# First stage of a hybrid block: weights in 256-column blocks, raw tiles in the input ring, state-space preparation moved forward

## The chip, the cores and the metric

The kernel runs on 1 core of one Trainium2 chip. The metric is the device time of one execution in microseconds; the median of the runs is compared. Engines are named as in the profile: PE (TensorE's matmuls), PEld (its weight loads), DVE (VectorE), ACT (ScalarE), POOL (GpSimd), SP (the engine that issues most DMAs; "SPq" is its queue).

## The reference

A decoder block on x (1024 tokens x 1024 channels) with 256 memory tokens. Cut to what matters here:

```python
u = rms_norm(h, norm_mix[l]);  proj = u @ w_in[l]
u_ssm, q, k, v, f_logit, gate_logits = jnp.split(proj, [...], axis=-1)   # u_ssm: 512 columns
y_ssm = gelu(s5_ssm(u_ssm, lam_re, lam_im, log_dt, b_re, b_im, c_re, c_im, d_skip))
# lam_bar = exp(lam * dt); b_bar = ((lam_bar - 1) / lam) * b; a scan over time; y = Re(C state) + D*u
...   # forgetting attention, gates, output projection
h = h + memory_cross_attention(rms_norm(h, norm_mem_q), rms_norm(mem, norm_mem_kv), w_mem_q, w_mem_kv, w_mem_o)
h = h + (silu(f_a) * f_b) @ w_ffn_out[l]
```

## The kernel before

All matmuls are done in three parts: each float32 operand is split into a rounded high part and the remainder (`split`, lines 177 to 179: a cast on ACT, then a subtraction on DVE, or on POOL where asked), and `mm3` (lines 166 to 170) adds high x high, high x low and low x high in PSUM.

The first stage, `stage_in`, does three things. It normalises two tiles of memory tokens ("m", "n") and eight tiles of x (128 tokens each), transposes them on PE (line 223) and splits the result into `mT` and `uT` (`turned`; its tiles are `mh`, `ml` and `uh`, `ul`). It multiplies the memory by `w_mem_kv`: keys transposed, one group of 128 columns at a time (K0 to K3), and values by two blocks of rows at a time (V0 to V3). And it multiplies x by the 512 state-space columns of `w_in`, transposed: four groups of 128 columns (q) by two halves of the tokens (h), the steps Uqh, each eight k-blocks of three matmuls. The results go to DRAM (`kv_d`, `u_d`).

Weights go through three steps. D*i* (`wget`) loads a tile of 128 x 1024 into one of two `raw` slots: for i = 0 to 3 all 1024 rows by 128 key columns, for 4 to 7 two row blocks by 512 value columns, for 8 to 11 (8, 9, a, b) all rows by 128 input columns. W*i* (`wsplit`) splits it into a pair `whi`, `wlo` (four slots of each; a "g" behind the step puts the subtraction on POOL). K, V or U reads it. The x tiles, memory tiles and gain rows share a ring of ten slots ("xt").

The state-space layer's preparation, class `S5`, is part of this stage. `load(0)` to `load(3)` are the steps L0 to L3: L0 loads lambda, the step sizes and the two C matrices, L1 loads the two B matrices and d_skip, L2 and L3 transpose lambda and C on PE. `prepare` is a generator whose parts are the steps P0 to P5: exponentials (P0), sine and cosine (P1), tables `la` and `ld` (P2), `bb` from B (P3), and `cb` and the d_skip product (P4). The scratch tiles of the sine, and `tb` of P3, share the two slots of the tag `craw` with the C matrices.

What sets the order: a list of steps, `ORDER_IN`, is written out by hand (F: fetch a tile, Q: sum of squares, R: root, S: scale, T: transpose half a tile, E: evacuate and split it, G: gain row, X: warm-up matmuls, u/k/v: outputs). It is the order of priority, not of execution. The framework's planner goes through the program with a time for each instruction of its own, and gives each engine and SP's queue a fixed order: of what is ready by its reckoning, what is listed first. Slots of a tag are waited for by semaphores. `B.behind(ins)` makes what is issued in its block, on the engine of `ins`, follow `ins` in that engine's order.

The second stage, `stage_ssm`, runs 32 gate columns of 24 matmuls on PE (`gate`, `gate_weights`, two blocks of weights for two column groups, loaded by `wblock`, line 153) and weaves the four quarters of the state-space layer between them: `turn_weights(q)` before column 4 + 7q (its transposes are line 1351), `states(q)` before 5 + 7q (line 1382, which reads `xg`, loaded at line 1375), `out(q)` before 9 + 7q. `weights(q)` makes `fre`, `fim` and `Gm` from `ld`, `la`, `bb` and `cT` on POOL and DVE (lines 1300 to 1319), and the doubling of `EC`, `ES` on POOL and, for the upper levels, DVE (lines 1332 to 1334).

Of the kernel before, what the change touches and what calls it, by code (L numbers as in the profile page):

```python
# [9 lines left out]
F32 = mybir.dt.float32  # L10
# [4 lines left out]
ALU = mybir.AluOpType  # L15
# [4 lines left out]
P = 128  # L20
D = 1024
L = 1024
NT = 8
GRP = 32
NH = 8
DH = 64
ML = 256
# [4 lines left out]
RAW = 1072  # L32
# [34 lines left out]
def f32(ap):  # L67
    return ap.bitcast(F32)
# [50 lines left out]
class Block:  # L119
# [55 lines left out]
            self.mm3(ps, wh[:, k0 + k, :], wl[:, k0 + k, :], rh, rl, k == 0, k == nk - 1)  # L175

    def split(self, hi, lo, src, pool_lo=False):
        self.A.copy(hi, src)  # L178
        (self.G if pool_lo else self.V).tensor_sub(lo, src, f32(hi))  # L179
# [46 lines left out]
    def turned(self, ps, b, act, t):  # L226
        for i in range(0, 4, act.kg):
            hi, lo = act.tok(4 * b + i, t, act.kg)
            self.split(hi, lo, ps[:, i * P:(i + act.kg) * P].rearrange("p (k c) -> p k c", k=act.kg))

    def norm_turn(self, xs, act, t):

# [101 lines left out]
def stage_in(B, xp, s5, x, mem, g_mix, g_kv, w_in, w_mem_kv, uT, u_d, kv_d):  # L334
# [14 lines left out]

    def fetch(t):  # L350
        tiles[t] = xtile()
        S.dma_start(tiles[t], mem[(t + 2) * P:(t + 3) * P, :] if t < 0 else x[t * P:(t + 1) * P, :])

    def gain_rows():

# [29 lines left out]
        ps[t, b] = B.turn(tiles[t], b, ("misc", "pv")[b])  # L385

    def evac(t, b):
        B.turned(ps.pop((t, b)), b, *((mT, t + 2) if t < 0 else (uT, t)))

    def wget(i):  # L390
        if i < 4:
            src = w_mem_kv[:, i * P:(i + 1) * P]
        elif i < 8:
            src = w_mem_kv[2 * (i - 4) * P:2 * (i - 3) * P, 512:1024]
        else:
            src = w_in[:, C_U + (i - 8) * P:C_U + (i - 7) * P]
        raw[i] = B.wpool.tile([P, RAW], F32, tag="raw", bufs=2, name="raw")[:, :D]
        raw["last"] = S.dma_start(raw[i].rearrange("p (k c) -> p k c", k=D // src.shape[-1]),
                                  src.rearrange("(k p) c -> p k c", p=P))

    def wsplit(i, pool):
        hl = [B.wpool.tile([P, WSLOT], F32R, tag=t_, name=t_)[:, :D] for t_ in ("whi", "wlo")]
        if i < 8:
            B.split(*hl, raw.pop(i), pool)
        else:

            B.split(*[t_.rearrange("p (k n g) -> p k n g", k=8, n=16) for t_ in hl],
                    raw.pop(i).rearrange("p (k g n) -> p k n g", k=8, g=8), pool)
        w[i] = [t_.rearrange("p (k c) -> p k c", k=2 if 4 <= i < 8 else 8) for t_ in hl]
# [719 lines left out]
class S5:  # L1129
# [9 lines left out]
    def load(self, part):  # L1139

        B, sp = self.B, self.sp
        lam_re, lam_im, log_dt, b_re, b_im, c_re, c_im, d_skip = self.raw
        V, T, S, ident = B.V, B.T, B.S, B.ident
# [4 lines left out]
        if part == 0:  # L1148
            self.rows = sp.tile([48, P], F32, name="prow")
            S.dma_start(self.rows[0:16, :], lam_re.rearrange("(j two) p -> j (two p)", two=2))  # L1150
            S.dma_start(self.rows[16:32, :], lam_im.rearrange("(j two) p -> j (two p)", two=2))
            self.ldr = sp.tile([48, 2], F32, name="ldr")
            S.dma_start(self.ldr[32:48, :], log_dt.rearrange("(j two) -> j two", two=2))
            self.craw = []
# [4 lines left out]
            return  # L1159
        if part == 1:  # L1160
# [15 lines left out]
        for t_, cr in zip(self.cT, self.craw):  # L1176
            ps = B.bank("misc")
# [4 lines left out]
                B.A.copy(t_[64 * two:64 * two + 64], pv[:, two])  # L1182

    def prepare(self):
        B, sp, bb, dbc, par = self.B, self.sp, self.braw, self.dbc, self.par
# [61 lines left out]
        V.tensor_mul(t1, xr, li)  # L1247
        V.tensor_sub(qi, qi, t1)
        V.tensor_mul(qi, qi, den)
        self.bb = [pt("bb_re", [16, 16]), pt("bb_im", [16, 16])]  # L1250
        tb = sp.tile([P, 256], F32, tag="craw", bufs=2, name="tb").rearrange("p (j n) -> p j n", j=16)
        bc = lambda q_: q_.unsqueeze(2).to_broadcast([P, 16, 16])
# [5 lines left out]
        V.tensor_add(self.bb[1], self.bb[1], tb)  # L1258
        yield

        self.cb = [pt("cb_re", [16, 2, 16]), pt("cb_im", [16, 2, 16])]
        for i in range(2):
            G.memset(self.cb[i], 0.0)
            for g in range(2):
                V.tensor_scalar(out=self.cb[i][64 * g:64 * g + 64, :, g, :], in0=self.cT[i][64 * g:64 * g + 64],
                                scalar1=1.0 if i == 0 else -1.0, scalar2=None, op0=ALU.mult)
# [5 lines left out]
        self.dm = dbc.rearrange("p (g m) -> p g m", g=GRP)  # L1272
        V.tensor_tensor(out=self.dm, in0=self.dm,
                        in1=msk.unsqueeze(1).to_broadcast([P, GRP, 16]), op=ALU.mult)

    def t2(self, name, bufs=1):
        return self.qp.tile([P, 512], F32, tag=f"q_{name}", bufs=bufs, name=name)
# [554 lines left out]
```

## Time and profile before

| | us |
|---|---|
| median of 3 runs (1605.04 to 1607.14) | 1605.51 |
| the profiled execution | 1608.0 |
| its span, first to last instruction | 1606.3 |
| PE busy in the span | 1549.5 |
| DVE, ACT, POOL busy | 1025.3, 657.7, 252.8 |
| mean granted clock of TensorE | 0.981 |

A row of a timeline has start, length, engine, line, operation, tiles out<-in, shapes and count; what stands in brackets is how long the engine stood idle before it and what ended that. A row of the waits has who waited, for whom, the total in us, how many times, and the longest. The chain of work is followed back from the last instruction of the stretch asked for; each piece has start, length and what it was.

### The profile page before, as it was taken

How to read it: one execution, taken by the hardware profiler on the slowest of the kernel's cores; microseconds unless marked ns; L12 is line 12 of the kernel's file. 1: busy time of each engine (PE TensorE's matmuls, PEld its weight loads, DVE VectorE, ACT ScalarE, POOL GpSimd, SP SyncE). 2: the span in 40 equal slices, each digit the busy share in tenths (PEclk: the TensorE clock that was granted, in tenths of full speed). 3: DMA queues.
4: the chain of work that ended last, by engine and by line, in shares of the span. 5: the costliest groups of instructions: out<-in, count | busy, mean ns of one | idle time of the engine just before them, and what ended most of it. 6: DMA issues, size and time to landing. Idle time of an engine off the chain costs nothing.

```text
span 1606.3 us, 20464 instructions
## 1 busy us (share of the span) xinstructions
PE 1549.5 (96%) x7323; PEld 1272.1 (79%) x7323; DVE 1025.3 (64%) x1850; ACT 657.7 (41%) x1179; POOL 252.8 (16%) x336
## 2 busy tenths in 40 slices
PE   8698989999999999999999999999999999999997
PEld 6587878898877668888888787888888888788886
DVE  7645563425678786767555687876776677565555
ACT  6432333332466564223335564333333333344342
POOL 2007545010121112320001210100100000000001
PEclk9898999999999999999999999999999999999999
DMA  7743344663022554538603168444455544796642
GB/s 241 139 104 65 80 132 107 134 169 64 2 49 53 125 139 140 182 116 271 229 1 106 53 221 297 151 151 157 157 165 162 164 151 147 271 391 226 196 157 105
DMA packets 197625, 239.82 MB, mean 149 GB/s; under 512 B 35386, under 2 KB 126426, under 8 KB 197012
## 3 DMA queue, kind: packets, MB, share of 16 engines
q1 hardware_dynamic: 190900, 222.80, 47.2%
q10 hardware_dynamic: 6624, 15.73, 2.5%
q8 instruction: 57, 0.93, 0.3%
q14 instruction: 44, 0.36, 0.1%
HBM read 164.56 MB, written 75.86 MB: 150 GB/s over the span
## 4 chain that ended last, share of the span: by engine, by line
PE 79%; DVE 6%; DMA 5%; issue 4%; POOL 3%; ACT 2%; SPq 1%; DVEq 0%; POOLq 0%; ACTq 0%
PE mm L886 15%; PE pv L886 7%; PE mm L168 7%; PE mm L170 7%; PE mm L169 7%; PE mm L1023 5%; PE sc L886 4%; PE sc L1023 4%; PE pv L1023 3%; PE sc L168 3%; PE sc L170 3%; PE sc L169 3%; PE misc L1023 2%; DMA raw<-in_w_in_dram 2%; PE pv L168 1%
## 5 line engine op out<-in xcount | busy, mean ns | idle before, releaser
L179 DVE TENSOR_TENSOR wlo<-raw,whi 128x1024 fp32r<-128x1024 f32 (+2 forms) x121 | 130.1, 1078 | 139.6 <-ACT whi L178 138.3
L178 ACT CAST whi<-raw 128x1024 fp32r<-128x1024 f32 (+2 forms) x124 | 116.4, 940 | 217.7 <-DMA raw<-in_w_ffn_in_dram 55.2
L168 PE MATMUL mm<-uh,whi 128*128 128x512 f32 x344 | 139.5, 405 | 2.9 <-ACT whi L178 2.8
L169 PE MATMUL mm<-ul,whi 128*128 128x512 f32 x344 | 137.5, 400 | 0.0
L170 PE MATMUL mm<-uh,wlo 128*128 128x512 f32 x344 | 136.9, 398 | 0.0
L179 DVE TENSOR_TENSOR ol<-or,oh 128x1024 fp32r<-128x1024 f32 x73 | 89.3, 1223 | 70.1 <-ACT oh L178 69.1
L178 ACT CAST oh<-or 128x1024 fp32r<-128x1024 f32 x73 | 76.8, 1053 | 102.6 <-PE pv L1023 33.7
L918 POOL TENSOR_TENSOR g<-a,c 128x512 f32<-128x512 f32 x22 | 35.5, 1613 | 392.1 <-ACT a L917 392.1
L168 PEld LDWEIGHTS mm<-uh,whi 128*128 128x128 f32 x344 | 66.6, 194 | 15.9 <-ACT whi L178 3.3
L170 PEld LDWEIGHTS mm<-uh,wlo 128*128 128x128 f32 x344 | 66.1, 192 | 14.9 <-DVE wlo L179 1.3
L1651 POOL TENSOR_TENSOR pl<-pf,ph 128x512 fp32r<-128x512 f32 (+1 forms) x32 | 37.8, 1181 | 245.9 <-DVE ph L1650 200.9
L169 PEld LDWEIGHTS mm<-ul,whi 128*128 128x128 f32 x344 | 66.4, 193 | 11.3
L197 POOL TENSOR_TENSOR r<-ms,mhalf 128x1 f32<-128x1 f32 x26 | 16.1, 621 | 353.2 <-DVE ms L193 344.0
L1648 ACT ACTIVATE pf<-sc 128x512 f32<-128x512 f32 (+1 forms) x96 | 46.5, 490 | 50.4 <-DVE sc L1644 30.5
L886 PE MATMUL pv<-S3h,we 128*128 128x512 f32 x176 | 58.1, 389 | 0.0
L168 PE MATMUL sc<-uh,whi 128*128 128x512 f32 x104 | 41.5, 399 | 0.0
L1023 PE MATMUL mm<-oh 128*128 128x512 f32 x106 | 41.2, 389 | 0.0
L1023 PE MATMUL mm<-ol,oh 128*128 128x512 f32 x106 | 41.2, 389 | 0.0
L1023 PE MATMUL mm<-oh,ol 128*128 128x512 f32 x106 | 41.2, 389 | 0.0
L170 PE MATMUL sc<-uh,wlo 128*128 128x512 f32 x104 | 41.0, 395 | 0.0
L169 PE MATMUL sc<-ul,whi 128*128 128x512 f32 x104 | 41.0, 394 | 0.0
L168 PE MATMUL mm<-yh,whi 128*128 128x512 f32 x104 | 40.8, 392 | 0.0
(585 smaller groups left out, 4561.6 us busy)
## 6 DMA issues: line engine op xcount, KB each, us to landing
or<-c_d SPq DMA_DIRECT2D x77, 256.0 KB
raw<-in_w_in_dram SPq DMA_DIRECT2D x22, 512.0 KB
wo<-in_w_ffn_out_dram SPq DMA_DIRECT2D x22, 512.0 KB
c_d<-g SPq DMA_DIRECT2D x44, 256.0 KB
t_d<-wo SPq DMA_DIRECT2D x44, 256.0 KB
or<-t_d SPq DMA_DIRECT2D x44, 256.0 KB
raw<-in_w_ffn_in_dram SPq DMA_DIRECT2D x20, 512.0 KB
rawb<-in_w_ffn_in_dram SPq DMA_DIRECT2D x20, 512.0 KB
```

The lines of the kernel that those rows point to most:

```text
L168: T.matmul(ps, lh, rh, start=first, stop=False)
L169: T.matmul(ps, lh, rl, start=False, stop=False)
L170: T.matmul(ps, ll, rh, start=False, stop=last)
L178: self.A.copy(hi, src)
L179: (self.G if pool_lo else self.V).tensor_sub(lo, src, f32(hi))
L197: self.G.tensor_tensor(out=r, in0=v, in1=self.mhalf[:, 0:n], op=ALU.pow)
L886: T.matmul(ps, l_[:, k, :], r_, start=first and k == 0 and i == 0, stop=k == 3 and i == 2, skip_group_check=True)
L918: G.tensor_mul(g[:, 512:], a1, c1)
L1023: T.matmul(ps, l_[:, gi], r_[:, 512:], start=n < 3 and p == 0 and k == 0 or n == 7 and p == 0 and k == 0, stop=p == NP - 1 and k == 2, ski ...
L1648: self.exp = A.activation(pf[:, off:], ps[:, off:], AF.Exp)
L1651: G.tensor_sub(pl[:, off:], pf[:, off:], f32(ph[:, off:]))
```

## The change

Four things are changed, all in the first stage.

- Key weights (D0 to D3) and input weights (D8 to Db) are loaded as blocks of 512 rows by 256 columns instead of 1024 rows by 128 columns. Two tiles together hold two groups of columns; `column` takes the k-block from the first or the second. Rows of a load are 1 KB instead of 512 bytes.
- The raw tiles of the input weights take slots of the x tiles' ring instead of the two raw slots.
- Each weight split carries an edge: its cast on ACT follows the cast of the evacuation listed last before it.
- L0 loads lambda and the step sizes alone, and follows the last x tile's load instead of a weight's; the C matrices move to L1. `cb` and the d_skip product follow the last operation of `bb` on DVE. `prepare` reads B later, so that it may be started before L1.

`ORDER_IN` is written anew:

```diff
-Fm g Fn X16 D0 G0 X6 Qm Qn Rm D1 Sm F1 Tm0 Rn Em0 Sn Tn0 F0 Tm1 W0 Q0 G1 Tn1 En0 F2 Q1 W1g En1 Em1 K0 D2 F3 K1 R0
-S0 T00 T01 k0 E00 Q2 W2g D3 E01 F4 F5 D4 S1 T10 Q3 W3 k1 D5 K3 K2 W4 E10 W5 F7 D6 R1 F6 k2 T11 k3 S2 Q4 V0 S3g T30
-E11 D7 Q5 T20 R2 T21 E21 E20 S4 E30 W6 W7 T40 V1 D8 D9 L0 S5 E40 W8 T31 V2 T41 E31 V3 Da T50 Q6 v T51 W9
-E51 U00 Q7 E41 R3 S6 u00 Db L1 T60 E50 S7 T61 T70 Wag E61 U10 L2 E60 P0 U20 u10 T71 E70 E71 u20 P1 U21 U11 Wb U30
-P2 u30 U31 u11 u31 U01 L3 u21 P3 P4 P5 u01
+Fm g Fn X16 D0 G0 X6 Qm Qn Rm D1 Sm F1 F0 Tm0 Rn Em0 Sn Tn0 F2 Tm1 W0 Q0 F3 G1 Tn1 En0 F4 Q1 W1g En1 Em1 K0 D2 F5 K1 R0
+S0 T00 T01 k0 E00 Q2 W2g D3 E01 F7 F6 L0 S1 T10 Q3 W3 k1 D4 K3 K2 D5 E10 W4 D8 D9 R1 k2 T11 k3 S2 Q4 W5 V0 Da S3g T30
+E11 D6 Q5 T20 R2 T21 E21 E20 S4 E30 D7 L2 T40 V1 S5 E40 W6 W7 T31 V2 Db L1 T41 E31 V3 W8 W9 T50 Q6 v U00 T51
+E51 Q7 E41 P0 R3 S6 u00 U10 T60 E50 S7 T61 u10 P1 T70 E61 Wa Wbg E60 T71 U20 E70 E71 u20 U21 P2 U11 L3 U30
+P3 u30 U31 u11 u31 U01 u21 P4 P5 u01
...
     def split(self, hi, lo, src, pool_lo=False):
-        self.A.copy(hi, src)
+        cast = self.A.copy(hi, src)
         (self.G if pool_lo else self.V).tensor_sub(lo, src, f32(hi))
+        return cast
...
     def evac(t, b):
-        B.turned(ps.pop((t, b)), b, *((mT, t + 2) if t < 0 else (uT, t)))
+        ps["turned"] = B.turned(ps.pop((t, b)), b, *((mT, t + 2) if t < 0 else (uT, t)))
...
         if i < 4:
-            src = w_mem_kv[:, i * P:(i + 1) * P]
+            src = w_mem_kv[512 * (i % 2):512 * (i % 2 + 1), 256 * (i // 2):256 * (i // 2 + 1)]
...
-            src = w_in[:, C_U + (i - 8) * P:C_U + (i - 7) * P]
-        raw[i] = B.wpool.tile([P, RAW], F32, tag="raw", bufs=2, name="raw")[:, :D]
+            src = w_in[512 * (i % 2):512 * (i % 2 + 1), C_U + 256 * (i // 2 - 4):C_U + 256 * (i // 2 - 3)]
+        raw[i] = xtile("raw") if i > 7 else B.wpool.tile([P, RAW], F32, tag="raw", bufs=2, name="raw")[:, :D]
...
     def wsplit(i, pool):
         hl = [B.wpool.tile([P, WSLOT], F32R, tag=t_, name=t_)[:, :D] for t_ in ("whi", "wlo")]
+        with B.behind(ps.get("turned")):
...
+    def column(i, o, act, h, out):
+        for k in range(8):
+            rh, rl = act.rhs(k, h)
+            wh, wl = [t_[:, k % 4, o * P:(o + 1) * P] for t_ in w[i + k // 4]]
+            B.mm3(out, wh, wl, rh, rl, k == 0, k == 7)
+
     def keys(h):
         ps["k", h] = B.bank("mm")
-        B.gemm_t(ps["k", h][:, :ML], *w[h], mT, 0, 8)
+        column(h // 2 * 2, h % 2, mT, 0, ps["k", h][:, :ML])
...
     def ssm_in(q, h):
         ps["u", q, h] = B.bank("mm")
-        B.gemm_t(ps["u", q, h], *w[8 + q], uT, h, 8)
+        column(8 + q // 2 * 2, q % 2, uT, h, ps["u", q, h])
...
     def params(i):
-        with B.behind(raw["last"] if i < 2 else None):
+        with B.behind(raw["last"] if i == 1 else tiles["last"] if i == 0 else None):
             s5.load(i)
```

More of the change, by code (lines that the diff above doesn't have):

```diff
@@ L228, in turned @@
             hi, lo = act.tok(4 * b + i, t, act.kg)
-            self.split(hi, lo, ps[:, i * P:(i + act.kg) * P].rearrange("p (k c) -> p k c", k=act.kg))
+            last = self.split(hi, lo, ps[:, i * P:(i + act.kg) * P].rearrange("p (k c) -> p k c", k=act.kg))
+        return last
     def norm_turn(self, xs, act, t):
@@ L351, in fetch @@
         tiles[t] = xtile()
-        S.dma_start(tiles[t], mem[(t + 2) * P:(t + 3) * P, :] if t < 0 else x[t * P:(t + 1) * P, :])
+        tiles["last"] = S.dma_start(tiles[t], mem[(t + 2) * P:(t + 3) * P, :] if t < 0 else x[t * P:(t + 1) * P, :])
     def gain_rows():
@@ L402, in wsplit @@
         hl = [B.wpool.tile([P, WSLOT], F32R, tag=t_, name=t_)[:, :D] for t_ in ("whi", "wlo")]
[L403 to L409, printed above, removed]
+        with B.behind(ps.get("turned")):
+            if i < 8:
+                B.split(*hl, raw.pop(i), pool)
+            else:
+                B.split(*[t_.rearrange("p (k n g) -> p k n g", k=8, n=16) for t_ in hl],
+                        raw.pop(i).rearrange("p (k g n) -> p k n g", k=8, g=8), pool)
+        w[i] = [t_.rearrange("p (k c) -> p k c", k=2 if 4 <= i < 8 else 4) for t_ in hl]
+    def column(i, o, act, h, out):
[3 more added lines that the diff above has]
+            B.mm3(out, wh, wl, rh, rl, k == 0, k == 7)
     def keys(h):
         ps["k", h] = B.bank("mm")
-        B.gemm_t(ps["k", h][:, :ML], *w[h], mT, 0, 8)
+        column(h // 2 * 2, h % 2, mT, 0, ps["k", h][:, :ML])
     def keys_out(h):
@@ L1153, in load @@
             S.dma_start(self.ldr[32:48, :], log_dt.rearrange("(j two) -> j two", two=2))
+            return
+        if part == 1:
             self.craw = []
@@ L1158, in load @@
                 self.craw.append(cr)
-            return
-        if part == 1:
             self.braw = [pt("b_re", [16, 16]), pt("b_im", [16, 16])]
@@ L1184, in prepare @@
     def prepare(self):
-        B, sp, bb, dbc, par = self.B, self.sp, self.braw, self.dbc, self.par
+        B, sp, par = self.B, self.sp, self.par
         V, A, G = B.V, B.A, B.G
@@ L1249, in prepare @@
         V.tensor_mul(qi, qi, den)
+        bb = self.braw
         self.bb = [pt("bb_re", [16, 16]), pt("bb_im", [16, 16])]
@@ L1257, in prepare @@
         V.tensor_tensor(out=tb, in0=bb[0], in1=bc(qi), op=ALU.mult)
-        V.tensor_add(self.bb[1], self.bb[1], tb)
+        last = V.tensor_add(self.bb[1], self.bb[1], tb)
         yield
@@ L1264, in prepare @@
             for g in range(2):
-                V.tensor_scalar(out=self.cb[i][64 * g:64 * g + 64, :, g, :], in0=self.cT[i][64 * g:64 * g + 64],
-                                scalar1=1.0 if i == 0 else -1.0, scalar2=None, op0=ALU.mult)
+                with B.behind(last):
+                    V.tensor_scalar(out=self.cb[i][64 * g:64 * g + 64, :, g, :], in0=self.cT[i][64 * g:64 * g + 64],
+                                    scalar1=1.0 if i == 0 else -1.0, scalar2=None, op0=ALU.mult)
         msk = pt("msk", [16])
@@ L1271, in prepare @@
                         channel_multiplier=1)
-        self.dm = dbc.rearrange("p (g m) -> p g m", g=GRP)
-        V.tensor_tensor(out=self.dm, in0=self.dm,
-                        in1=msk.unsqueeze(1).to_broadcast([P, GRP, 16]), op=ALU.mult)
+        self.dm = self.dbc.rearrange("p (g m) -> p g m", g=GRP)
+        with B.behind(last):
+            V.tensor_tensor(out=self.dm, in0=self.dm,
+                            in1=msk.unsqueeze(1).to_broadcast([P, GRP, 16]), op=ALU.mult)
     def t2(self, name, bufs=1):
```

## The prediction

> **What bounds the kernel now.** I read the page first, then the windows of busy time, then the waits of PE, and last the chain of work and the engines' timelines at each hole.
>
> ```profile
> span 1606.3 us, 20464 instructions
> ...
> PE 1549.5 (96%) x7323; PEld 1272.1 (79%) x7323; DVE 1025.3 (64%) x1850; ACT 657.7 (41%) x1179; POOL 252.8 (16%) x336
> ```
>
> PE is busy for 1549.5 of 1606.3 us, so an edit that leaves PE's work alone can win only PE's holes, and time in which PE runs below its clock. The windows below are cut at the holes of the first two stages; the columns are the stretch, its length, the busy time of each engine (with instructions), and then PE's granted clock, DMA share and GB/s.
>
> ```profile
> 19.70:51.00 31.30, 29.07 (x180) 25.50 (x180) 28.02 (x68) 20.36 (x40) 5.05 (x2) 0.95 0.65 177
> 51.00:59.17 8.17, 0.00 (x0) 0.03 (x1) 2.37 (x3) 4.31 (x5) 0.00 (x0) 0.71 0.38 88
> 59.17:64.71 5.54, 5.54 (x17) 4.71 (x18) 5.25 (x12) 2.25 (x6) 0.00 (x0) 0.50 0.81 189
> ...
> 69.66:72.36 2.70, 0.01 (x2) 0.04 (x1) 2.70 (x4) 0.86 (x2) 1.09 (x3) 1.00 0.92 110
> ...
> 77.55:79.48 1.93, 0.00 (x0) 0.03 (x1) 1.43 (x4) 0.37 (x1) 0.00 (x0) 1.00 0.92 223
> 79.48:114.10 34.62, 34.62 (x157) 28.41 (x158) 13.39 (x64) 7.84 (x14) 0.00 (x0) 1.00 0.42 96
> 114.10:136.94 22.84, 22.84 (x105) 18.40 (x102) 16.80 (x74) 7.74 (x13) 10.47 (x36) 1.00 0.45 116
> 136.94:139.75 2.81, 0.14 (x1) 0.14 (x2) 2.74 (x4) 1.35 (x2) 2.73 (x4) 1.00 0.00 0
> 139.75:143.13 3.38, 0.90 (x5) 0.50 (x4) 2.30 (x3) 0.58 (x1) 3.24 (x3) 0.50 0.20 78
> 143.13:150.00 6.87, 6.87 (x26) 6.30 (x27) 2.28 (x4) 0.58 (x1) 4.33 (x4) 0.50 0.00 0
> ...
> 201.17:205.32 4.15, 0.00 (x0) 0.03 (x1) 2.60 (x3) 1.39 (x3) 2.59 (x3) 0.91 0.96 363
> 205.32:211.50 6.18, 6.18 (x23) 5.60 (x24) 4.00 (x6) 3.12 (x9) 2.48 (x3) 0.51 0.33 122
> ```
>
> The first stage ends on PE at 114.10, where the last input column ends and the gates' matmuls begin. Inside it PE stands still for 8.17, 2.69 and 1.93 us. After the longest hole it runs 5.54 us at clock 0.50, so half of that, 2.77, is lost too. The second stage has two more places: 136.94 to 150.00 (idle 2.67 and 2.48; 0.90 and 6.87 us at half clock, lost 3.9), and 201.17 (4.15 idle, then 6.18 us at 0.51, lost 3.0). PE's waits name what ended each hole:
>
> ```profile
> PE misc L223 <- DVE ul L179: 10.1, 2, 8.2
> ...
> PE pv L1382 <- DMA xg<-u_d: 4.2, 1, 4.2
> PE pv L223 <- DVE xt L217: 2.7, 1, 2.7
> PE pv L1351 <- POOL fre L1302: 2.7, 1, 2.7
> ```
>
> The 8.2 is a transpose of an x tile that waits for VectorE to empty a bank. VectorE was not working then: the chain of work, and its own row, say what it stood behind.
>
> ```profile
> 44.26 10.57 DMA raw<-in_w_in_dram
> ...
> 54.86 1.91 ACT whi L178
> ...
> 72.19 6.10 DMA dbc<-in_d_skip_dram
> ...
> 78.31 0.69 DVE dbc L1273
> ```
>
> ```profile
> 56.80 1.89 DVE L179 TENSOR_TENSOR wlo<-raw,whi 128x1024 fp32r<-128x1024 f32 x1 [7.78 <-ACT whi L178]
> ```
>
> A raw slot came free at 44.26; only then could the input weight W8 be loaded, and it took 10.57 us. ACT's cast of it and VectorE's subtraction (7.78 idle) stood at the heads of their queues, with the x tiles' evacuations behind them. The 1.93 is the same with another load: VectorE's d_skip product waits for `dbc`, which landed at 78.29. So three of the holes are loads that came late, in front of work that was ready.
>
> **The loads move (stage 1).**
>
> ```profile
> 30.03 0.38 SPq L398 DMA_DIRECT2D raw<-in_w_mem_kv_dram  x1
> ```
>
> W8 to Wb get slots of the x tiles (the ring of ten, which serves them in turn as memory and x tiles are transposed) instead of the two raw slots; they no longer wait for W6 and W7. The order lists D8 and D9 just after D5, which SP could issue at 30.03, so they go out some 13 us earlier and the 10.57 lie beside the key and value matmuls. The evacuations are listed ahead, and every weight cast now carries an edge behind the last evacuation before it on ACT, so a late weight can't block an x tile again. The d_skip product goes behind the last `bb` operation. Removed: 8.17 + 2.77 + 2.69 + 1.93 = 15.6 us. The other 2.23 idle in 19.70:51.00 I leave. The eigenvalue loads pass D4 to D9 on SP. D4's raw slot is free only when POOL has split W2 (below: 23.22 + 2.39 us), so I put them at nothing; without that cover D4 would be late by the time that SP spends on them, a few us.
>
> What this gives back, each term with its ends:
>
> ```profile
> 9.69 1.04 ACT L178 CAST whi<-raw 128x1024 fp32r<-128x1024 f32 x1 [0.53 <-DMA raw<-in_w_mem_kv_dram]
> ...
> 16.71 0.58 ACT L178 CAST mh<-misc 128x512 fp32r<-128x512 f32 x1 [1.98 <-PE misc L223]
> 17.68 1.07 ACT L374 ACTIVATE junk<-xt 128x1024 bf16<-128x1024 f32 x1
> ...
> 20.42 0.58 PE L169 MATMUL mm<-ml,whi 128*128 128x256 f32 x1 [0.22 <-DVE ml L179]
> ...
> 23.22 2.39 POOL L179 TENSOR_TENSOR wlo<-raw,whi 128x1024 fp32r<-128x1024 f32 x1 [8.48 <-ACT whi L178]
> ...
> 44.29 0.71 PE L168 MATMUL sc<-whi,mh 128*128 128x512 f32 x2
> ...
> 46.40 0.37 ACT L178 CAST uh<-misc 128x256 fp32r<-128x256 f32 x1 [1.29 <-PE misc L223]
> ```
>
> 1. *Keys.* A key column now needs two tiles, W0 and W1, and their casts stand behind the first evacuations. W0 was cast at 9.69; from 16.71 ACT has to do two evacuations (0.58), two squares (1.07) and two casts (1.04), 5.4 us, and POOL's subtraction of W1 takes 2.39: W1 is ready at 24.5. The first half of K0 (12 matmuls, 20.42 to about 23) covers most of the wait. I take 1.5, between 0 and 4.1 (24.5 - 20.4).
> 2. *Values.* W6 and W7 now stand behind E40. V2 began at 44.29; if E40's cast stays at 46.40, W6 is ready 0.4 + 1.05 + 1.2 later, at about 49, which is 4.7 late; if the transpose comes as early as its scaled tile allows, nothing. I take 2.0.
> 3. *First input column.* U00 needs W8 and W9, a cast and a subtraction more (1.91 and 1.89 by the rows of W8). The second pair hides behind U00's first 12 matmuls. I take 1.0, between 0 and 3.8.
> 4. *Preparation beside the x tiles.* VectorE has spare time after 51 now, and less then. Its rows:
>
> ```profile
> 63.26 0.76 DVE L179 TENSOR_TENSOR ul<-pv,uh 128x256 fp32r<-128x256 f32 x2
> ...
> 70.94 1.27 DVE L217 SCALAR_TENSOR_TENSOR xt<-xt,r,gain 128x1024 f32<-128x1024 f32 x1
> ```
>
> ```profile
> 82.39:92.10 9.71, 9.71 (x45) 8.04 (x46) 8.86 (x59) 1.23 (x3) 0.00 (x0) 1.00 0.01 3
> 114.50:124.10 9.60, 9.60 (x46) 7.69 (x45) 9.29 (x31) 4.91 (x9) 1.24 (x4) 1.00 0.79 180
> ```
>
> Before U21 it must do two weight subtractions (3.8), seven evacuations (5.3), two scales (2.5) and about 2.2 of value evacuations and roots: 13.8. Step P0, which is the window 82.39:92.10 (two evacuations are in it, which I leave in), adds up to 8.86: 22.7 in all. The cover is U00, U10 and U20; four gate columns and little else fill 22.84, so a column is 5.5, three are 16.5, and with the transposes between them some 19. That is 3.7 over if all of P0 falls there, less if part of it fills VectorE's 3.3 us of idle time before 51 (28.02 busy of 31.30). I take 2.0, between 0 and 8.9.
>
> Stage 1 thus ends 15.6 - 6.5 = 9.1 us sooner, at about 105. PE's arithmetic is the same: the same eight columns of 24 matmuls.
>
> **The preparation moves (stage 2).**
>
> ```profile
> 114.58 0.28 DVE L270 TENSOR_SCALAR trg_k<-mt 128x224 f32<-128x224 f32 x1 [3.75 <-PE misc L1179]
> ...
> 132.24 0.29 DVE L1332 TENSOR_TENSOR d<-EC,trg_cs 128x128 f32<-128x128 f32 x1 [5.16 <-POOL ES L1334]
> ```
>
> ```profile
> 141.88 1.19 POOL L1302 TENSOR_TENSOR fim<-w,w 128x448 f32<-128x448 f32 x1
> ```
>
> The sine's first tile sits in a slot of `craw`, so it waits for the transposes of the C matrices (step L3), which stood at the very end of the stage. From 114.58 to 143.07 the chain to `fim` takes 28.5 us, and PE has gates for 22.84: hence the two holes. The new order puts L3 behind U11, three columns ahead of the end: 16.5 us. `fim` is then ready 12 us after the stage's end instead of 28.5, 10.8 before PE wants it. The C loads move behind Db on SP with those of B and d_skip, but Db itself, no longer waiting for W9's split, goes out earlier too. I take the whole 2.67 + 2.48 + 3.9 = 9.0; the ends are 0 (L3 planned where it was) and 9.0.
>
> The hole at 201 is a load as well:
>
> ```profile
> 193.04 1.51 SPq L153 DMA_DIRECT2D raw<-in_w_in_dram  x2
> 194.64 0.46 SPq L1375 DMA_DIRECT2D xg<-u_d  x1
> ```
>
> `xg` stood on SP behind two gate loads that waited for VectorE, which was late with the first quarter's states. Of 4.15 + 3.0 = 7.2 I take 2.9, since that lateness partly comes from the first hole; ends 0 and 7.2. Gate weights now get slots only when U31 and U01 are done: one column (5.5) hides a cast and two subtractions (3.4).
>
> **The sum.** 9.1 + 9.0 + 2.9 = 21.0. The profiled execution took 1608.0 us (span 1606.3 and 1.7 around it), so its like would take 1587.0. It lies 2.5 above the median of the runs, 1605.51, so I forecast 1584.5 for the median.
>
> A rule weighs on the give-backs. A hole of 2.67 us (from 136.94) was enough here: from 139.75 on the clock is 0.50 for 10.25 us. The leftovers of 1 to 2 us I count without it. The Trainium skill (TensorE: Matmul & The Clock Gate, Part 1) gives half rate only after an idle window of about 3.4 us, and by it none of these leftovers could cost more than itself. By the trace one of them might, for up to 5.1; that end goes into the range.
>
> **Rivals.** *VectorE becomes the bound* (0.22). The loads are early, but P0 to P2 all stand ahead of the last evacuations: 8.9 + about 10 (the second window, its weight subtraction out, and the tables) against the 5.6 that the cover leaves. U21 waits 13 us, stage 1 wins nothing or loses 2, and the gain is stage 2's: 1605.5 - 9 = 1596. For it: 28.02 of 31.30 busy before 51. Against: P1 waits for L3, listed behind U11.
>
> *Slower* (0.16): the same place, with the doubling. If the planner also puts the first quarter's doubling ahead of the last evacuations, VectorE stands in order for POOL's part (5.16 in the row at 132.24), and runs the upper levels itself until about 142, 9.9 more. With P0, P1, P2 and `bb` (8.9, 10 and 3) that is 37 us ahead of U21; 31 of it PE waits, and 5 more are lost at half clock. Stage 1 then loses 25 and stage 2 wins 12: 1605.5 + 13 = 1618.5. It turns to a loss from about 24 us of preparation in front.
>
> *Nothing in sum* (0.05): the casts' edges bring back the stall in stage 1 and the S5 chain shifts with the stage: 1605.
>
> **How the numbers follow.** The forecast has 0.57. All bounds at their best give 15.6 + 2.2 + 9.0 + 7.2 = 34, that is 1571. Upward the range takes in the second case and a half clock on top of it, 1601. Slower and nothing, together 0.21, are left out. A difference under 0.2%, 3.2 us, can't be told from none. Faster 0.79, within 0.2% 0.05, slower 0.16.
>
> **What would show it.** Right: no wait of ACT for `raw<-in_w_in` in stage 1, no hole over 3 us between 20 and 105, the first `sc` gate matmul at about 105, L1351 without a wait, `xg` issued closer behind the first quarter's output. Wrong: PE L223 waiting for VectorE at 70 to 80 (rival one), or VectorE's L1332 ahead of the last `ul` (rival two), or the sine (L270) still at the stage's end.

## The result: 7 us faster, a third of what was forecast

| | us |
|---|---|
| before, median of 5 runs (1605.04 to 1607.14) | 1605.51 |
| after, median of 5 runs (1597.25 to 1600.66) | 1598.55 |
| ratio after/before, 95% interval | 0.9957 [0.9942, 0.9971] |
| forecast (range) | 1584.5 (1571 to 1601) |
| profiled execution, before and after | 1608.0 and 1598.55 |

The direction was right and the time lies in the range, but the size was not: 7.0 us came where 21 were expected. The page of the kernel after:

```profile
span 1596.8 us, 20467 instructions
...
PE 1542.6 (97%) x7323; PEld 1265.9 (79%) x7323; DVE 1026.5 (64%) x1850; ACT 657.1 (41%) x1179; POOL 254.3 (16%) x336
```

To see where the time went, both traces are cut at the same three marks of the program: the last input column's end, the first quarter's and the third quarter's `xg` matmuls. The first stage is cut besides at 19, 48 and 66 us of each trace. Windows of busy time, before:

```profile
19.00:48.00 29.00, 26.32 (x172) 23.41 (x170) 27.14 (x64) 21.00 (x41) 5.05 (x2) 0.94 0.61 187
48.00:66.00 18.00, 9.82 (x39) 7.96 (x38) 9.03 (x23) 6.83 (x11) 0.00 (x0) 0.72 0.68 143
66.00:114.29 48.29, 43.67 (x202) 35.42 (x201) 23.10 (x77) 14.62 (x25) 3.81 (x4) 1.00 0.55 107
...
114.10:154.10 40.00, 34.84 (x154) 28.73 (x152) 27.96 (x85) 10.26 (x16) 24.27 (x47) 0.87 0.30 76
154.10:254.46 100.36, 95.87 (x481) 81.50 (x480) 49.51 (x72) 34.53 (x56) 54.15 (x106) 0.97 0.50 117
```

And after, the same columns:

```profile
19.00:48.00 29.00, 21.88 (x136) 19.96 (x135) 26.41 (x59) 20.51 (x42) 8.17 (x3) 0.82 0.65 203
48.00:66.00 18.00, 15.51 (x69) 12.16 (x69) 16.81 (x39) 10.68 (x18) 0.00 (x0) 0.91 0.89 208
66.00:116.63 50.63, 47.00 (x210) 38.02 (x209) 28.93 (x128) 13.73 (x24) 4.64 (x3) 0.97 0.21 63
...
116.63:146.58 29.95, 29.95 (x146) 25.16 (x145) 12.18 (x15) 9.64 (x13) 23.85 (x53) 1.00 0.46 128
146.58:245.56 98.98, 94.52 (x482) 80.49 (x481) 56.85 (x83) 34.65 (x56) 52.92 (x102) 0.98 0.51 117
```

The second stage gave what was forecast: from its first gate to the third quarter it took 40.00 + 100.36 = 140.4 us before and 29.95 + 98.98 = 128.9 after, 11.4 less (forecast 11.9). The first stage gave nothing: the first gate comes at 116.6 instead of 114.3, where about 105 was forecast. (The profiled executions lie 9.5 apart, the medians 7.0.)

For the first stage I count what PE loses after 19 us in each part: its idle time (length less busy time), and half of its busy time inside the stretches at clock 0.50. The PEclk column is a mean that takes in idle time, so it falls lower than this second number alone would make it.

| lost, idle + half clock (us) | 19 to 48 | 48 to 66 | 66 to the end | sum |
|---|---|---|---|---|
| before | 2.7 + 1.6 | 8.2 + 2.7 | 4.6 + 0 | 19.8 |
| forecast for after | 5.8 | 3.0 | 2.0 | 10.8 |
| after | 7.1 + 4.2 | 2.5 + 1.7 | 3.6 + 1.7 | 20.8 |

The forecast's line is the line of before, less the 15.6 that go, plus the 6.5 of the give-backs, each in its part. The old stall at 48 to 66 did go. The new losses stand in front of it and behind it. Who was waited for, by PE's waits after (19 to 230 us):

```profile
PE pv L1439 <- ACT Tt L1383: 2.8, 1, 2.8
PE mm L170 <- POOL wlo L179: 2.8, 1, 2.8
PE sc L168 <- ACT whi L178: 2.3, 1, 2.3
PE pv L1396 <- DMA xg<-u_d: 1.6, 1, 1.6
PE mm L168 <- ACT uh L178: 1.4, 1, 1.4
PE misc L224 <- DVE rt L203: 1.4, 1, 1.4
PE mm L168 <- ACT whi L178: 1.2, 1, 1.2
```

No load stands here but `xg`. `Tt` and `xg` belong to the second stage; of the first stage's five rows three are weights being split (`wlo`, `whi`), 6.3 us of 9.1. Behind them, from the timelines of ACT, POOL and SP:

```profile
31.28 1.05 ACT L178 CAST whi<-raw 128x1024 fp32r<-128x1024 f32 x1
...
54.99 5.80 ACT L178 CAST whi<-raw 128x1024 fp32r<-128x1024 f32 x4
...
77.51 3.79 ACT L178 CAST whi<-raw 128x1024 fp32r<-128x1024 f32 x2
81.18 0.40 ACT L178 CAST uh<-misc 128x256 fp32r<-128x256 f32 x1
```

```profile
32.41 3.42 POOL L179 TENSOR_TENSOR wlo<-raw,whi 128x1024 fp32r<-128x1024 f32 x1 [7.80 <-DMA raw<-in_w_in_dram]
```

```profile
35.86 0.39 SPq L401 DMA_DIRECT2D raw<-in_w_mem_kv_dram  x1
```

The cast at 31.28 is W2, held by its edge until E00 is done. Its low part ends at 35.8, only then is its raw slot free, and D4 goes out at 35.86; before, W2's subtraction ended at 25.6 (the row at 23.22 in the prediction) and D4 followed it. W6 to W9 come as four casts in one piece at 54.99, behind E40. At 77.51 two casts with their edge satisfied stand in front of an evacuation (81.18): the block that the edges were to prevent, the other way round.

### The profile page after: what moved, and what is told of

Same layout as the page of the kernel before. It is cut to its first block, busy times and chain, and to the rows that moved or that the text cites. A ratio compares the mean times of both kernels' runs of the same rounds, so it can differ in the third digit from the quotient of the medians.

```text
span 1596.8 us, 20467 instructions
## 1 busy us (share of the span) xinstructions
PE 1542.6 (97%) x7323; PEld 1265.9 (79%) x7323; DVE 1026.5 (64%) x1850; ACT 657.1 (41%) x1179; POOL 254.3 (16%) x336
## 4 chain that ended last, share of the span: by engine, by line
PE 80%; DVE 7%; issue 4%; DMA 3%; POOL 3%; ACT 2%; SPq 1%; DVEq 0%; POOLq 0%; ACTq 0%
PE mm L897 15%; PE pv L897 7%; PE mm L168 7%; PE mm L170 7%; PE mm L169 7%; PE mm L1034 5%; PE sc L897 4%; PE sc L1034 4%; PE sc L169 3%; PE sc L170 3%; PE sc L168 3%; PE pv L1034 3%; PE misc L1034 2%; PE pv L168 1%; PE pv L170 1%
## 5 line engine op out<-in xcount | busy, mean ns | idle before, releaser
L169 PEld LDWEIGHTS mm<-ul,whi 128*128 128x128 f32 x344 | 65.6, 191 | 11.3
L1668 DVE TENSOR_TENSOR pl<-pf,ph 128x512 fp32r<-128x512 f32 (+2 forms) x64 | 35.1, 550 | 10.2 <-ACT ph L1667 9.4
L1129 POOL TENSOR_TENSOR sg<-sg,ga 128x512 f32<-128x512 f32 x16 | 29.4, 1858 | 73.4 <-DVE sg L1122 73.4
```

The source lines that it names most:

```text
L169: T.matmul(ps, lh, rl, start=False, stop=False)
L1129: self.B.G.tensor_mul(self.out[j][:, cs], self.out[j][:, cs], ga)
L1668: V.tensor_sub(pl[:, off:], pf[:, off:], f32(ph[:, off:]))
```

## The experiments

Theory A was that the edges cost what the loads gave; rival B the 256-column blocks (two tiles for each key column); rival C the preparation on VectorE, ahead of the last x tiles. Ratios are to the kernel before in the same runs.

**1. The edges off**, in the kernel after:

```diff
-        with B.behind(ps.get("turned")):
+        with B.behind(None):
```

> The changed kernel without the edge that puts a weight's cast behind the last evacuation (no weight has it). Theory A (the edges ate the gain of stage 1): W0 is cast near 10 us again and W2 near 23 instead of 31.28, D4 is issued near 26 instead of 35.86, the holes at 33.12 (2.8) and 53.83 (2.3) and the half clocks after them go, stage 1 ends near 108 instead of 116.8: about 1590 us. Theory B (the 256-column blocks cost it, because a key column now needs two tiles): the hole at 33 stays whatever the order on ACT is, 1597 to 1599. Theory C (VectorE is the bound of stage 1): the holes move but their sum stays, 1596 to 1600.

Measured: 1594.97, ratio 0.9935 [0.9921, 0.9948]; the interval overlaps that of after. First gate at 110.75, parts 4.4 + 4.1, 2.9 + 1.7, 3.0 + 0, sum 16.0 against 20.8. So the edges cost about 4.8 us in the profile and 3.6 in the median, less than half of the 8.5 that theory A gave. A wait of 3.0 for VectorE stays at 74.5, in the last part:

```profile
66.00:110.75 44.75, 41.79 (x196) 34.30 (x195) 28.98 (x117) 10.37 (x22) 3.69 (x3) 1.00 0.18 48
```

**2. L3 alone**, in the kernel before (the token L3 behind U11):

```diff
-... P1 U21 U11 Wb U30 P2 u30 U31 u11 u31 U01 L3 u21 P3 P4 P5 u01
+... P1 U21 U11 L3 Wb U30 P2 u30 U31 u11 u31 U01 u21 P3 P4 P5 u01
```

> The kernel before with one token of the order moved: step L3 (the transposes of the C matrices) directly behind U11 instead of behind U01. Theory (the whole gain of the change is the earlier sine): stage 1 ends at 114 to 115 as before, the two waits of PE for fre and fim go, and the time is about 1596, 9 to 10 less than the kernel before. Rival (the C loads, B loads or the edges behind bb are needed for it as well): a wait for fim of over 2 us stays and less than 4 us are won, over 1601.

Measured: 1591.58, ratio 0.9912 [0.9898, 0.9925]. One moved token gives twice what the whole change gives, and 4 us more than was expected of it. The windows: no wait from the stage's end to the first quarter, and 126.7 us to the third quarter's `xg`, against 140.4 before.

```profile
112.78:142.70 29.92, 29.92 (x145) 25.16 (x145) 11.76 (x15) 8.70 (x12) 27.69 (x56) 1.00 0.38 104
142.70:239.46 96.76, 93.97 (x481) 80.36 (x481) 54.01 (x79) 34.75 (x56) 50.24 (x100) 0.98 0.53 121
```

**3. The ring's slots alone**, in the kernel before:

```diff
-        raw[i] = B.wpool.tile([P, RAW], F32, tag="raw", bufs=2, name="raw")[:, :D]
+        raw[i] = xtile("raw") if i > 7 else B.wpool.tile([P, RAW], F32, tag="raw", bufs=2, name="raw")[:, :D]
```

> The kernel before with one line changed: the raw tiles of the input weights in the x tiles' ring, blocks, order and edges as before. Theory (the load of W8 was the long hole): it is issued near 36 instead of 44.26, ACT does not wait for it, the hole of 8.17 us and the half clock after it go, stage 1 ends near 104; the sine moves with the stage's end, so the waits for fre and fim stay: about 1595. Rival (VectorE is the bound of stage 1): other holes take its place, stage 1 ends at 110 or later, over 1601.

Measured: 1602.93, ratio 0.9984 [0.9975, 0.9993], over 1601, as the rival had it. But the stage ends at 108.75, between the theory's 104 and the rival's 110 and 5.5 sooner than before. The sine still sits at its end, so the second stage's waits move along with it and stay. The third quarter's mark comes 5.8 sooner and the profiled execution is 7.1 shorter, but the median only 2.6: one profile against another is no better than that.

**4. Edges on the input weights only**, in the kernel after:

```diff
-        with B.behind(ps.get("turned")):
+        with B.behind(ps.get("turned") if i > 7 else None):
```

> The changed kernel with the edge on the input weights alone (W8 to Wb); key and value weights are free. Theory A (the edges on key and value weights ate the gain): as without any edge, about 1590; if the edge on the input weights does its work, not slower than without it. Theory B (256-column key blocks) and theory C (VectorE): 1596 to 1600.

Measured: 1600.06, ratio 0.9969 [0.9955, 0.9983]; parts 4.4 + 4.3, 2.9 + 1.7, 3.6 + 1.7, sum 18.6. In the first two parts it is the run without edges, in the last it is the kernel after: so with the edges on W8 to Wb 5.3 are lost behind 66 instead of 3.0, and those on W0 to W7 make about 2.2 ahead of it. Theory A had 1590 here and fails: the time is clear of run 1's and not below that of after, so by the times the edges on the input weights cost all that edges cost, and those on W0 to W7 nothing that shows.

**5. L3 and the slots together**: the edits of runs 2 and 3, in the kernel before.

> The kernel before with two parts of the change and no other: step L3 directly behind U11, and the raw tiles of the input weights in slots of the x tiles' ring. Alone, L3's place took 13.9 us off the time, and the slots took 5.4 us off the first stage and 2.6 off the whole. Theory A (the gains are these two, and what eats them are the edges and the order around them): the gains add, since with L3 early the second stage starts without a wait wherever the first stage ends; first gate matmul near 109, time 1591.6 - 4 = 1587.5, within 1586 to 1590. Rival (the slots' gain is taken back behind the first stage whatever the sine does): 1591, as with L3 alone.

Measured: 1590.88, ratio 0.9911 [0.9895, 0.9927]: as with L3 alone. The gains did not add in the median, though the first gate comes at 110.4 in the profile, against 113.3 in run 2; the clock in that profile is looked at in the last section.

**6. 128-column blocks again**, without the edges:

```diff
-            src = w_mem_kv[512 * (i % 2):512 * (i % 2 + 1), 256 * (i // 2):256 * (i // 2 + 1)]
+            src = w_mem_kv[:, i * P:(i + 1) * P]
...
-            src = w_in[512 * (i % 2):512 * (i % 2 + 1), C_U + 256 * (i // 2 - 4):C_U + 256 * (i // 2 - 3)]
+            src = w_in[:, C_U + (i - 8) * P:C_U + (i - 7) * P]
...
-        column(h // 2 * 2, h % 2, mT, 0, ps["k", h][:, :ML])
+        B.gemm_t(ps["k", h][:, :ML], *w[h], mT, 0, 8)
...
-        column(8 + q // 2 * 2, q % 2, uT, h, ps["u", q, h])
+        B.gemm_t(ps["u", q, h], *w[8 + q], uT, h, 8)
```

> The kernel after without the edges, and with the key and input weights in 128-column blocks again. Against the kernel after without the edges alone (1594.97, first gate matmul at 110.6, keys' end at 33.8). Theory A (the blocks cost little: a key column waits for two tiles once): keys end about 1.5 earlier, time within 1592 to 1596. Theory B (the 256-column blocks are what the change pays, since each column needs two casts and two subtractions): stage 1 ends at 106 to 107, time 1590 to 1591.

Measured: 1594.95, ratio 0.9938 [0.9922, 0.9955], the same as run 1. Rival B falls by the time: the part 19 to 48 loses 6.6 instead of 8.5, but 48 to 66 loses 8.3 instead of 4.6, and the first gate comes at 113.9, 3.2 later than in run 1.

**7. The edges alone**, in the kernel before:

```diff
+        with B.behind(ps.get("turned")):     # around both branches of the split
             if i < 8:
                 B.split(*hl, raw.pop(i), pool)
```

> The kernel before with the edges alone: each weight's cast follows the cast of the evacuation listed last before it. Theory A (the edges hold back casts of weights that have landed, and through the two raw slots the loads behind them): keys and values end later than before (35.5 and 51.0), by 3 to 10 us, the input weights load later, and the time is 1608 to 1615. Rival (an edge costs only where the order of the list puts it late, as with W2 in the new list): in the old list W2 also stands behind E00, but W4 to W9 behind E10 to E41; no measurable difference, 1604 to 1607.

Measured: 1613.03, ratio 1.0044 [1.0028, 1.0059]: 7 us slower by the ratio, as theory A said. The first gate comes at 123.7. D4 goes out at 37.8 instead of 25.6, and all loads behind it with it; ACT then waits 6.0 us for D8. PE's waits:

```profile
PE pv L224 <- DVE rt L202: 5.6, 1, 5.6
PE mm L168 <- ACT whi L178: 4.0, 1, 4.0
PE mm L169 <- DVE ul L179: 3.1, 1, 3.1
```

**8. P0 and P1 listed behind E71**, without the edges:

```diff
-E51 Q7 E41 P0 R3 S6 u00 U10 T60 E50 S7 T61 u10 P1 T70 E61 Wa Wbg E60 T71 U20 E70 E71 u20 U21 P2 U11 L3 U30
+E51 Q7 E41 R3 S6 u00 U10 T60 E50 S7 T61 u10 T70 E61 Wa Wbg E60 T71 U20 E70 E71 u20 P0 P1 U21 P2 U11 L3 U30
```

> The kernel after without the edges, and with the steps P0 and P1 (exponentials, sine and cosine) listed behind the last x tile's evacuation instead of ahead of the scales of tiles 6 and 7. Against the kernel after without the edges alone (1594.97; PE waits 3.0 us for VectorE's ul at 74.5). Theory C (VectorE is the bound there: P0 stands in front of the x tiles): the wait at 74.5 goes, stage 1 ends at 107 to 108, time 1591 to 1592. Theory A (the wait is the weight subtractions of W8 to Wb, not P0): the wait stays between 2 and 3.5, time 1594 to 1596, or later if the sine is then late for the second stage.

Measured: 1596.25, ratio 0.9944 [0.9929, 0.9959]. By its times this looks like theory A, but the edit had not done what it says: the timeline of VectorE has P0's last operation still in front of the subtraction that PE waits for.

```profile
75.45 0.17 DVE L1226 TENSOR_TENSOR em<-em,e 128x16 f32<-128x16 f32 x1
75.54 0.42 DVE L179 TENSOR_TENSOR ul<-misc,uh 128x256 fp32r<-128x256 f32 x1
```

A list of priorities moves nothing that is ready by the planner's reckoning while what should pass it is not. So run 8 says nothing on theory C, and it was made again with an edge. The new list did shift losses all the same: 48 to 66 loses 2.2 instead of run 1's 4.6, and behind 66 it is 7.6 instead of 3.0.

**9. The preparation held behind E71 on VectorE**, with run 8's list and without the weights' edges:

```diff
+        ps["low"] = B.low        # the evacuation's subtraction on VectorE
...
+    def prepare():
+        with B.behind(ps.get("low")):
+            next(prep, None)
```

> The kernel after without the edges on the weights, P0 and P1 listed behind the last x tile's evacuation, and the preparation's operations on VectorE held behind that evacuation's subtraction by an edge of their own: the list alone (the run before of this kind) had left them ahead of it, from 69.7 to 76.0. Theory C (P0 on VectorE is what PE waits for): the hole of 3.0 to 4.7 us at 72 to 77 goes or falls under 1, the first gate matmul comes at 107 to 108 instead of 110.6, and since VectorE then stood idle for 14 us before the sine, nothing is late behind it: 1591 to 1592.5. Theory A (the wait is the weight subtractions of Wa and Wb): a hole over 2 stays, 1594 to 1596.

Measured: 1587.39, ratio 0.9887 [0.9871, 0.9903], clear of run 1's interval, and faster than both kernels. Windows:

```profile
19.00:48.00 29.00, 24.64 (x146) 21.82 (x147) 24.71 (x62) 17.36 (x37) 5.24 (x2) 0.83 0.73 193
48.00:66.00 18.00, 15.84 (x76) 12.23 (x75) 17.71 (x32) 14.53 (x20) 2.74 (x1) 1.00 0.92 220
66.00:106.06 40.06, 39.92 (x188) 32.75 (x187) 29.32 (x130) 9.82 (x21) 2.05 (x3) 1.00 0.19 50
```

Behind 66 PE stands for 0.14 us in all. The first gate comes at 106.06, a microsecond from the forecast's 105, and the time is 2.9 above its 1584.5. The hole is gone, as theory C said; the time is 3.6 lower than theory C gave, which the hole alone does not explain. The sine was not late for it: in the kernel after VectorE had stood idle for 17.0 us in front of it, waiting for the C transposes until 99.87.

**10. D8 held behind D7 on the load queue**, on top of run 5:

```diff
+        with B.behind(raw["last"] if i == 8 else None):
             raw["last"] = S.dma_start(...)
```

> The kernel before with L3 directly behind U11, the input weights' raw tiles in the x ring's slots (1590.9, first gate matmul at 110.6), and the first input weight's load D8 held behind the last value weight's load D7 on the load queue. In the run without this, D8 passed D7, D7 landed at 52.1, and PE waited 3.4 and 0.8 us for the values' weights, 1.7 more lost at half clock. Theory A (the early input loads collide with the value weights' loads): both holes fall under 1 us, the first gate matmul comes at 105 to 107, and the time is 1586 to 1588. Rival (the values' weights are late whatever passes them, since the two raw slots come free late): the holes stay, 1590 to 1592.

Measured: 1586.79, ratio 0.9892 [0.9875, 0.9908], which overlaps run 5's. The value weights' two holes went; another of 5.5 us came, since ACT's cast of W8 now waits for D8 in front of evacuations. So it is in part luck that the time lies in theory A's range. The cast:

```profile
48.99 1.91 ACT L178 CAST whi<-raw 128x1024 fp32r<-128x1024 f32 x1 [5.67 <-DMA raw<-in_w_in_dram]
```

**11. The edge off W2 only**, in the kernel after:

```diff
+        with B.behind(ps.get("turned") if i != 2 else None):
```

> The kernel after, with the edge taken from one weight only, W2. Theory A (of the edges on key and value weights it is W2's, behind E00, that costs: it holds the raw slot that D4 wants): W2 is cast near 22 instead of 31.3, D4 to D7 go out 8 to 10 us earlier, keys end at about 34, values at about 61.5, the first gate matmul comes near 113.5, time as without the edges on W0 to W7: 1595 to 1596. Rival (the edges on W1, W3 and W4 to W7 hold as much): the keys end after 38 and the stage no earlier than 115.5, 1597 to 1599.

Measured: 1598.75, ratio 0.9955 [0.9940, 0.9969]. My expectation failed; the rival's numbers came. D4 goes out at 27.6 instead of 35.9, as said, and the keys end at 39.3 instead of 44.0, but the stage ends at 116.4: the value weights W6 and W7 are still behind E40 (a wait of 2.8 at 52.4), and PE's idle time in the last part is the same 3.6. An edge taken away shows nothing where the next one holds.

**12. Edges on W8 and W9 alone, where the weight is late**, on top of run 10:

```diff
-... S5 E40 W8 T31 V2 T41 E31 V3 Da T50 Q6 v T51 W9
+... S5 E40 T31 V2 T41 E31 V3 Da T50 Q6 v T51 W8 W9
...
+        with B.behind(ps["turned"] if i in (8, 9) else None):
```

> The kernel of the last run with D8 behind D7 (1586.8, first gate matmul at 107.5), with two edges more: the splits of W8 and W9 are listed behind V3 and their casts follow the evacuation listed last before them. In the run without them PE stood for 5.5 us at 48.4, because ACT's cast of W8 waited 5.7 us for D8 with evacuations of x tiles queued behind it, and 3.4 us were lost at half clock after that. Theory A (an edge pays where the weight it holds is late and the evacuation behind it is ready): the hole falls to 0 to 2 us, half of what it and its half clock cost comes off the stage, the first gate matmul at 103 to 105, time 1582 to 1585. Rival (the input weights are then what is late, so the hole moves to the first input column): first gate matmul at 106.5 to 108, time 1586 to 1588.

Measured: 1591.60, ratio 0.9913 [0.9890, 0.9935]: not better than run 10, and later than either theory. The hole of 5.5 did go, and one of 1.9 before the first input column and one of 3.9 before a scaled x tile came. The load is as late as it was; the edge moved the place where PE meets it.

**13. All edges on, the preparation held as in run 9**: that kernel with `B.behind(ps.get("turned"))` around the splits again.

> The kernel after with all its edges on the weights, and only the preparation held behind the last x tile's evacuation on VectorE (P0 and P1 also listed there). Theory (the edges' 6.0 us and the preparation's 4.6 us are separate costs that add): first gate matmul at 116.7 - 4.6 = 112, time 1598.6 - 7.6 = 1591. Rival (in the changed kernel the waits at 76 to 82 are all the casts of Wa and Wb, so moving P0 frees nothing there): first gate matmul at 115 to 117, time 1596 to 1599.

Measured: 1599.31, ratio 0.9955 [0.9937, 0.9973]: nothing gained. The last part:

```profile
66.00:114.59 48.59, 44.95 (x196) 36.24 (x195) 30.97 (x130) 13.86 (x24) 4.63 (x3) 0.93 0.19 56
```

It loses 3.6 + 2.8, no less than after. So the two costs do not add. Both stand in front of the same evacuations of the last x tiles, and whichever is there makes PE wait: with edges and preparation 5.3 is lost behind 66, with edges alone 6.4, with the preparation alone 3.0, with neither 0.1. The times say the same: 1598.55, 1599.31, 1594.97 and 1587.39.

**14 and 15. VectorE beside POOL**, on top of run 9: the scale of tile 3 off POOL, then the low parts of W1 and W2 too (tokens `S3g` to `S3`; `W1g`, `W2g` to `W1`, `W2`). In run 9 a root step that takes 0.16 us elsewhere lasts as long as POOL's product:

```profile
32.83 2.30 DVE L202 TENSOR_TENSOR rt<-r 128x2 f32<-128x2 f32 x1
```

```profile
32.73 2.39 POOL L216 TENSOR_TENSOR xt<-xt,gain 128x1024 f32<-128x1024 f32 x1 [5.08 <-ACT xt L215]
```

> The fastest kernel so far (after without the edges on the weights, preparation behind the last x tile's evacuation: 1587.4, first gate matmul at 106.1), with the scale of x tile 3 on VectorE instead of ScalarE and POOL. In that kernel's profile a 128x2 root step on VectorE (L202), 0.16 us elsewhere, lasts 2.30 from 32.83, while POOL's product of tile 3 runs from 32.73 to 35.12; PE then waits 2.28 us for the subtraction behind it, and the half clock from 38.9 to 45.7 costs 3.4 more. Theory D (VectorE stands while POOL works, and this is what is left of the keys' give-back): the hole and the half clock go, VectorE has 1.3 us more to do; 1.5 to 4.5 us off the stage, 1583 to 1586. Rival (the root step is long for another reason, or the half clock comes from the hole before it): the hole stays over 1.5 or another takes its place, 1586 to 1589.

> The same, with the low parts of W1 and W2 on VectorE too (1.22 us each there; 2.5 and 2.9 on POOL, beside which a root step took 2.33). Theory D: the holes of 0.8 before mm L170 and the early one go as well, 0 to 2 us less than with tile 3's scale alone: 1582 to 1586. Rival (VectorE, 24.7 of 29 us busy there, is then the bound): the first stage's keys end later, 1587 to 1590.

Measured: 1591.11, ratio 0.9913 [0.9893, 0.9933], and 1590.87, ratio 0.9916 [0.9892, 0.9939]: no gain, and above what theory and rival gave. With POOL's product away the root step takes 0.16 us and the 2.28 us hole is gone, so in run 9 it was the product that this step stood behind. Not everything on VectorE does: beside POOL's subtraction from 67.79 in the kernel before, two of the evacuations' subtractions took 0.42 and 0.41 us, and only the root step was long (2.00). PE met the value weights instead, for 3.3 us in run 14 and in run 15 for

```profile
PE sc L168 <- ACT whi L178: 4.8, 1, 4.8
```

From 19 to 66 us runs 9, 14 and 15 lose 11.0, 12.5 and 10.5 us, however the waits are dealt out. What sets that sum was not taken away in any run. The DMA share of run 9 in these parts is 0.73 and 0.92, against 0.61 and 0.68 before, and the value weights still pass through two raw slots; that the loads are the limit there is argued from this, not shown.

## Why the forecast was wrong, step by step

**The loads move: right.** ACT's wait for `raw<-in_w_in` and the wait for `dbc` are gone, and 48 to 66 loses 4.2 instead of 10.9. D8 went out at 27.54.

**Keys, 1.5: wrong by 5.5.** The part 19 to 48 loses 11.3 instead of 4.3. I costed W0 and W1 behind the first evacuations and took W2's low part from the row of before (23.22), though the edge holds W2 as well, behind E00. It was cast at 31.28, and PE waited 2.8 for it and lost 2.5 more at half clock (34.1 to 41.0). Without edges 8.5 are still lost; with one tile for a key column again (run 6) 6.6, but what that saves is lost again behind 48.

**Values and first input column, 2.0 and 1.0: size 4.2 instead of 3.0.** V2 waits 2.3 for W6 behind E40, as costed; the half clock after it (1.7) was left out. The 1.0 did not come: U00 starts at 64.26 without a wait.

**Preparation beside the x tiles, 2.0: wrong as a cause.** Behind 66 the stage loses 5.3 us. Taking the preparation away there does nothing while the edges stand (run 13), and gives the 3.0 of idle time back when they do not (run 9).

**The step that failed** stands in the part on the loads: "so a late weight can't block an x tile again" treats an edge as free. The sum has no term for the edge on W2, on whose slot D4 waits, and none for those on Wa and Wb. With its edge the cast of Wa comes late for PE (1.2 us), and the casts of Wa and Wb, bunched behind one evacuation, stand 3.79 us long in front of the next (1.4). So the 9.1 us of the first stage did not come: it ended 2.3 later.

**The second stage, 11.9: right,** 11.4 measured. L3's place gives all of it: run 2 has it alone. To the first quarter's `xg` 10.05 were saved (9.0 forecast; the 1.0 more is the C transposes, 1.07 us of PE, now in the first stage); of the 2.9 behind that 1.4 came, and a new wait of 2.8 for `Tt` stands at 170.3. `fim` is ready at 128.8 (started 127.66, 1.16 long), 12.2 behind the stage's end where 12 was forecast, and PE reads it at 138.8.

**The rule on the clock: the trace disagrees.** I had left the half clock out of the give-backs and kept "up to 5.1" for the range. The clock fell to 0.50 from 34.1 to 41.0, from 58.0 to 61.4 and from 81.9 to 85.3: the first time inside a hole of 2.8 us (from 33.1), the second 1.9 us after one of 2.3 (from 53.8), the third after holes of 1.1, 1.2 and 1.4 (from 76.6 on). In the whole stage, with a stretch at 20.5 that before has too, 7.6 us were lost so, 4.4 before. (The "up to 5.1" is half of 10.25 us, in which PE was busy for 7.8; what it cost there was 3.9.) By the Trainium skill (TensorE: Matmul & The Clock Gate, Part 1) none of these holes fills an idle window of about 3.4 us.

**The rivals.** The time came out near VectorE as the bound (1596), but not by its mechanism: VectorE's preparation was not what PE waited for in the kernel after, it would have been next. The rival nearest to the trace is the one I gave 0.05, casts' edges bringing the stall back in the first stage; only its second half, a shift of the S5 chain that eats the rest, did not come.

Of the 14 missing microseconds run 9 gives back 11.2 in the median and 9.7 in the profile (losses of 20.8 against 11.1). Of the 9.7, 5.2 lie behind 66: edges and preparation, two holds on the same evacuations, priced apart, and the edges there not at all. Another 2.5 lie at the keys and went with the edges. The last 2.0 lie between 48 and 66 and went in runs 8, 9 and 13 (2.2, 2.2 and 2.4 lost there), which list P0 and P1 further back; why, no run shows. With neither hold the first stage ends at 106.1 where the forecast had 105, but by luck in part: the keys lose 8.8 instead of 5.8, the other two parts 2.3 instead of 5.0.

## What to carry to other kernels

An ordering edge has a price, and it is paid by what is queued behind the held instruction: the slot that it frees, the load that waits for the slot, and the next item on its own engine. Two holds on the same wait must be taken away together, since one of them alone can look free: the preparation did in run 13. And look in the trace whether an edit of a priority list moved what it should before reading its time: run 8 had not.

## What the runs showed of the hardware

PE's own work does not settle when its clock first rises. Runs 5 and 10 have the same instructions in the same order on PE up to this place; in the timelines of the two, run 5 first:

```profile
11.94 2.07 PE L368 MATMUL sc<-grow,junk 1*128 1x512 f32 x2
...
20.48 0.63 PE L223 MATMUL pv<-ident,xt 128*128 128x128 f32 x2
```

```profile
11.79 1.12 PE L368 MATMUL sc<-grow,junk 1*128 1x512 f32 x2
...
17.23 0.38 PE L223 MATMUL pv<-ident,xt 128*128 128x128 f32 x2
```

PE starts the same work at the same time, twice as slowly in run 5, and ends the memory transposes 3.5 us later. At full speed a 128x256 matmul of the keys takes 0.28 us, at half 0.41; run 10 fell back between 18.4 and 21.8, run 5 first rose at 26.6. The Trainium skill (the same page and part) says that the window of the clock gate runs free of the kernel's start and that cold phases differ between runs, by half a microsecond in its words; here it was 15 us. In the seventeen profiled executions the rise came at 11.1 to 12.5 us in nine, at 16.9 to 17.8 in five and at 26.6 to 30.2 in three. Eight of the nine early ones are variants of the kernel after, and the three late ones variants of the kernel before, so the kernel may have a part in it; each kernel has one trace, and no run separates that from chance. The stage's end in one profile can't be compared with another's to better than some 3 us, and losses were counted from 19 us on, behind the rise in every run for which a sum is given. That single executions spread for this reason (run 10: 1585.25 to 1591.61) is argued, not shown. It also leaves the difference between runs 5, 10 and 12 open: their intervals overlap, and in the profiled executions runs 5 and 12 rose late and run 10 early.
